# Triangular inverses by 32-row diagonal blocks: 32-column stationary operands and vector-engine block transposes in place of full 128-wide steps

## The chip, the cores and the metric

The kernel runs on one core of one Trainium2 chip. The metric is device time in microseconds, the median of three runs.

## What is computed

The reference chains three transformer-like blocks over 512 tokens of 1024 channels. The change lies in the second one, in its two recurrences: a chunked gated delta rule (`gdn` in the kernel) and an RWKV-7 scan (`rwkv`), each with 8 heads and chunks of 128 tokens. Cut to what matters:

```python
# chunk_gated_delta_rule, per head and chunk of C = 128 tokens
lower = jnp.where(strict, jnp.einsum('bhncd,bhnsd->bhncs', k_beta, k) * decay, 0.0)
t_mat = lax.linalg.triangular_solve(lower + eye, jnp.broadcast_to(eye, lower.shape),
                                    left_side=True, lower=True, unit_diagonal=True)
u = jnp.matmul(t_mat, v_beta)
w = jnp.matmul(t_mat, k_beta * jnp.exp(g_cum)[..., None])
# rwkv7_scan, per head
S = S * w_t[:, :, None, :] + sa[..., None] * b_t[:, :, None, :] + v_t[..., None] * k_t[:, :, None, :]
y_t = jnp.einsum('bhvk,bhk->bhv', S, r_t)        # sa = S a_t
```

The kernel brings the RWKV scan into the same chunked form, so both need, for each head, the inverses of four unit lower triangular 128x128 matrices I + L, one per chunk.

## The kernel before

Most of the program is linear layers. `lin` (L358) makes one 128-row output tile over 512 tokens: for each of its 128x128 weight blocks three matmuls (L368 to L370), since weights and activations are split into a high and a low part; the weight pieces come by DMA on SP and are split on ACT (L324) and DVE (L325). All work is written as calls of engines, and the framework's scheduler turns it at build time into one fixed order per engine; a section under `first()` goes ahead of other work, and two generators given to `run` are advanced in turn.

`second` (L1145) loops over j = 0 to 3, two heads each. For each j, `z.run(rwkv(...), gdn(...))` (L1231) advances the two chains in turn. Beside them the scheduler puts matmuls of `lin`: the layers of the next j (`lins`, called L1246) and gates whose results `aside` stores (L1248; 2, 1, 1 and 12 of them in j = 0 to 3). The RWKV chain has tiles `ra`, small tiles `mra` and three PSUM banks `r`; the GDN chain has `ga`, `mga` and two banks `g`.

Each chain calls `Chain.invert` (L680) once per head (L1379, L1489), so a j has four inversions and the program 16. One inversion takes `Lt`, a 128x512 tile of four transposed strictly lower matrices side by side, and leaves the four transposed inverses in `Tt`. It doubles the size b of the inverted diagonal blocks, over b = 2, 4, 8, 16, 32: a copy of the odd columns of `Lt` on ACT (L703), two matmuls with it as stationary operand (L707), a mask on DVE (L711), two matmuls with the transposed inverse as stationary operand (L714), a subtraction on DVE (L716), and then `turned`: a copy of the odd columns on ACT (L695), two transposes on TensorE (L655) and a copy out of PSUM on ACT (L659). The last step, from 64 to 128, is two groups of four 64x64 matmuls (L727, L734) with a DVE operation behind each (L730, L736).

## Time and profile before

| | |
|---|---|
| runs | 3328.02, 3328.61, 3330.11 us |
| profiled execution | 3330.9 us, of which span 3329.1 us |
| mean granted TensorE clock | 0.992 |
| busy: PE, PE weight loads, DVE, ACT, POOL | 97%, 81%, 67%, 45%, 3% |
| instructions in the span | 48326 |

The profile shows one execution. PE is TensorE's matmul stream, PEld its weight loads, which overlap with matmuls; DVE, ACT and POOL are the vector, scalar and GpSimd engines. The end of a matmul is modelled, with a tail that overlaps the next, so the time a matmul costs is read from one start to the next. One fp32 matmul leaves two records (two passes), a transpose one.

### The profile page before, as it was taken

How to read it: one execution, taken by the hardware profiler on the slowest of the kernel's cores; microseconds unless marked ns; L12 is line 12 of the kernel's file. 1: busy time of each engine (PE TensorE's matmuls, PEld its weight loads, DVE VectorE, ACT ScalarE, POOL GpSimd, SP SyncE). 2: the span in 40 equal slices, each digit the busy share in tenths (PEclk: the TensorE clock that was granted, in tenths of full speed). 3: DMA queues.
4: the chain of work that ended last, by engine and by line, in shares of the span. 5: the costliest groups of instructions: out<-in, count | busy, mean ns of one | idle time of the engine just before them, and what ended most of it. 6: DMA issues, size and time to landing. Idle time of an engine off the chain costs nothing.

```text
span 3329.1 us, 48326 instructions
## 1 busy us (share of the span) xinstructions
PE 3242.3 (97%) x19041; PEld 2700.3 (81%) x19041; DVE 2234.4 (67%) x3675; ACT 1497.2 (45%) x2491; POOL 101.0 (3%) x186
## 2 busy tenths in 40 slices
PE   7999999999999999999999999999999999999998
PEld 6778888888887887887888887888877778888887
DVE  5696645986578577566887567777687996363344
ACT  6443433432346656654332334645546665232222
POOL 0000000000000000000000000000000001000000
PEclk9999999999999999999999999999999999999999
DMA  4223333665332112125367324222227567423332
GB/s 134 64 70 98 95 117 102 215 202 161 107 103 76 46 50 73 58 64 171 122 203 242 95 81 133 69 78 92 81 80 239 171 208 239 131 88 101 95 95 76
DMA packets 128324, 393.33 MB, mean 118 GB/s; under 512 B 16056, under 2 KB 23480, under 8 KB 128096
## 3 DMA queue, kind: packets, MB, share of 16 engines
q1 hardware_dynamic: 113776, 346.82, 33.6%
q0 software_dynamic: 13168, 42.36, 3.7%
q8 instruction: 150, 2.46, 0.3%
q10 hardware_dynamic: 1152, 1.05, 0.1%
q14 instruction: 78, 0.64, 0.1%
HBM read 358.44 MB, written 31.74 MB: 117 GB/s over the span
## 4 chain that ended last, share of the span: by engine, by line
PE 88%; DVE 6%; ACT 4%; issue 2%; DMA 1%; SPq 0%; POOL 0%; DVEq 0%; ACTq 0%; POOLq 0%
PE mm L368 20%; PE mm L369 20%; PE mm L370 20%; PE mm L354 3%; PE mm L355 3%; PE mm L356 3%; PE s L2082 1%; DVE wl L325 1%; PE s L2068 1%; ACT wh L324 1%; PE r L1370 1%; PE g L655 1%; PE mm L405 1%; PE r L655 1%; PE mm L406 1%
## 5 line engine op out<-in xcount | busy, mean ns | idle before, releaser
L368 PE MATMUL mm<-h,wh 128*128 128x512 f32 x2400 | 947.6, 395 | 1.8 <-ACT t L948 1.5
L369 PE MATMUL mm<-h,wh 128*128 128x512 f32 x2400 | 948.5, 395 | 0.0
L370 PE MATMUL mm<-h,wl 128*128 128x512 f32 x2400 | 947.3, 395 | 0.0
L324 ACT ACTIVATE wh<-wr 128x1024 fp32r<-128x1024 f32 x464 | 491.4, 1061 | 949.8 <-PE mm L369 663.5
L325 DVE TENSOR_TENSOR wl<-wr,wh 128x1024 fp32r<-128x1024 f32 x464 | 567.2, 1224 | 467.6 <-ACT wh L324 462.2
L368 PEld LDWEIGHTS mm<-h,wh 128*128 128x128 f32 x2400 | 452.7, 189 | 98.4 <-issue 5.5
L370 PEld LDWEIGHTS mm<-h,wl 128*128 128x128 f32 x2400 | 452.7, 189 | 96.9 <-issue 6.0
L369 PEld LDWEIGHTS mm<-h,wh 128*128 128x128 f32 x2400 | 452.8, 189 | 96.2 <-issue 5.4
L368 PE MATMUL mm<-p,wh 128*128 128x512 f32 x599 | 233.6, 390 | 0.0
L369 PE MATMUL mm<-p,wh 128*128 128x512 f32 x599 | 233.4, 390 | 0.1
L370 PE MATMUL mm<-p,wl 128*128 128x512 f32 x599 | 233.1, 389 | 0.0
L354 PE MATMUL mm<-h,wh 128*128 128x256 f32 (+1 forms) x480 | 159.5, 344 | 14.4 <-DVE t L1930 5.3
L355 PE MATMUL mm<-h,wh 128*128 128x256 f32 (+1 forms) x480 | 160.1, 339 | 1.1 <-DVE h L569 1.0
L356 PE MATMUL mm<-h,wl 128*128 128x256 f32 (+1 forms) x480 | 158.6, 335 | 0.0
L301 DVE SCALAR_TENSOR_TENSOR ac<-wa,adas,ac 128x1024 f32<-128x1024 f32 x98 | 125.5, 1282 | 23.9 <-DMA wa<-wa 23.5
L369 PEld LDWEIGHTS mm<-p,wh 128*128 128x128 f32 x599 | 112.4, 188 | 23.9 <-DVE p L430 0.8
L368 PEld LDWEIGHTS mm<-p,wh 128*128 128x128 f32 x599 | 112.4, 188 | 23.5
L370 PEld LDWEIGHTS mm<-p,wl 128*128 128x128 f32 x599 | 112.4, 188 | 23.4
L354 PEld LDWEIGHTS mm<-h,wh 128*128 128x128 f32 x480 | 92.4, 198 | 25.8 <-ACT h L568 4.6
L355 PEld LDWEIGHTS mm<-h,wh 128*128 128x128 f32 x480 | 94.3, 198 | 10.0 <-DVE h L569 2.0
L356 PEld LDWEIGHTS mm<-h,wl 128*128 128x128 f32 x480 | 94.6, 198 | 8.5
L750 DVE SCALAR_TENSOR_TENSOR f<-mm,par,f 128x511 f32<-128x511 f32 (+1 forms) x128 | 95.5, 746 | 1.1
(661 smaller groups left out, 5244.6 us busy)
## 6 DMA issues: line engine op xcount, KB each, us to landing
wr<-w SPq DMA_DIRECT2D x464, 512.0 KB, 3.7
wa<-wa SPq DMA_DIRECT2D x96, 512.0 KB, 4.3
e<-cum SPq DMA_DIRECT2D x64, 256.0 KB, 5.1
x<-x POOLq DMA_DIRECT2D x40, 256.0 KB, 4.5
s<-ecum SPq DMA_DIRECT2D x64, 128.0 KB, 4.8
cd<-t POOLq DMA_DIRECT2D x24, 256.0 KB, 2.3
gt<-t POOLq DMA_DIRECT2D x16, 256.0 KB, 2.5
fr<-gt SPq DMA_DIRECT2D x16, 256.0 KB, 3.0
```

The source lines that it names most:

```text
L301: self.V.scalar_tensor_tensor(a, raw, s[:, k, m:m + 1], a, op0=ALU.mult, op1=ALU.add)
L324: self.A.activation(hi, raw, AF.Copy)
L325: self.V.tensor_tensor(lo, raw, hi.bitcast(F32), op=ALU.subtract)
L354: self.T.matmul(ps[:, n], lhsT=wh, rhs=x[0][k][:, n], start=k == 0, stop=False)
L355: self.T.matmul(ps[:, n], lhsT=wh, rhs=x[1][k][:, n], start=False, stop=False)
L356: self.T.matmul(ps[:, n], lhsT=wl, rhs=x[0][k][:, n], start=False, stop=k == last)
L368: self.T.matmul(out, lhsT=wh, rhs=x[0][k], start=k == 0, stop=False)
L369: self.T.matmul(out, lhsT=wh, rhs=x[1][k], start=False, stop=False)
L370: self.T.matmul(out, lhsT=wl, rhs=x[0][k], start=False, stop=k == last)
L405: self.T.matmul(ps, lhsT=a, rhs=wl, start=False, stop=False)
L655: self.z.T.transpose(ps[:, c * P:(c + 1) * P], src[:, c * P:(c + 1) * P], self.z.ident)
L750: z.V.scalar_tensor_tensor(out[:, d:], src[:, :S - d], w[:, n - 1 - d:n - d], out[:, d:], op0=ALU.mult, op1=ALU.add)
```

## The change

`invert` is written anew up to the last step. Only the four 32x32 diagonal blocks of each matrix are worked on while b goes through 2, 4, 8, 16. The blocks of all four matrices together are one 128x128 tile `Tc`, one matrix per 32 columns; `Tb` holds the same blocks, turned, as block diagonals in a 128x512 tile whose other elements were set to zero on POOL (L716). In a level `right` does four matmuls with 32 columns of `Tc` as stationary operand and 128 columns of `Lb` moving (L704), each to its own 32 partitions of PSUM; DVE turns the 32x32 blocks of the result with its own transpose (L706); `left` does four matmuls with 32 columns of that as stationary operand and `Tb` moving (L713); DVE masks (L733), turns (L734) and subtracts (L735); `turned` transposes `Tc` once on TensorE (L697) and copies it in four pieces of 32 rows into `Tb` on ACT (L699). For the step from 32 to 64 `right` is done once more, four POOL multiplies (L744) spread the blocks into the result `Tt`, which lies in the place of `Lb`, `left` is done for blocks 1 and 3 alone, two ACT copies (L749) put them into `Tt`, and a small tile `first`, made by DVE and three ACT copies (L751 to L755), is the moving operand of the first 64x64 group (L761). The two 64x64 groups stay (L761, L768). The chains get two more small tiles each (`ira`, `iga`). Line numbers of this section are those of the changed kernel, where `invert` begins 2 lines lower than before and ends 34 lines lower.

```diff
@@ -145,10 +145,12 @@
     c.add("eps_x", np.full((P, 1), 64e-5, f))
     c.add("incl", (r[None] >= r[:, None]).astype(f))
     c.add("strict", (r[None] > r[:, None]).astype(f))
-    c.add("m1", ((r[None] % 2 == 1) & (r[:, None] == r[None] - 1)).astype(f))
-    g = np.arange(64)
-    for b in (2, 4, 8, 16, 32):
-        c.add(f"lev{b}", (r[:, None] // b == r[None] // b).astype(f))
+    l, g = r[:, None] % 32, np.arange(32)[None]
+    c.add("id32", (l == g).astype(f))
+    for b in (1, 2, 4, 8, 16):
+        c.add(f"lev{b}", ((l // b % 2 == 0) & (l // b == g // b - 1)).astype(f))
+    c.add("lev32", (r[:, None] // 32 == r[None] // 32).astype(f))
+    c.add("off32", ((r[:, None] // 32 % 2 == 0) & (r[:, None] // 32 == r[None] // 32 - 1)).astype(f))
     c.add("rs128", np.broadcast_to((np.arange(S) % 128 != 0).astype(f), (P, S)))
     rs16 = np.broadcast_to((np.arange(S) % 16 != 0).astype(f), (P, S))
     c.add("inclT", (r[None] <= r[:, None]).astype(f))
@@ -679,54 +681,86 @@
 
     def invert(self, Lt, out):
 
         z, V, A, T = self.z, self.z.V, self.z.A, self.z.T
         quad = lambda x: x.rearrange("p (u n) -> p u n", u=4)
-        Tt, Ti = self.t(), self.t()
+        cut = lambda x: x.rearrange("p (u i n) -> p u i n", u=4, i=4)
+        bc = lambda x: x.unsqueeze(1).to_broadcast([P, 4, x.shape[1]])
+        rows = [slice(32 * i, 32 * i + 32) for i in range(4)]
+        small = lambda n=P: z.tile("m" + self.sb, n)
+        Lb, Tb, Tc = self.t(), self.t(), z.tile("i" + self.sb, P)
+        Tt = Lb
         out.append(Tt)
-        bc = lambda x, n: x.unsqueeze(1).to_broadcast([P, 4, n])
-        V.tensor_tensor(quad(Tt), quad(Lt), bc(z.k("m1"), P), op=ALU.mult)
-        V.tensor_tensor(quad(Tt), bc(z.ident, P), quad(Tt), op=ALU.subtract)
-        self.transposes(Tt, Ti)
+        def turned(ps):
+            T.transpose(ps, Tc, z.ident)
+            for u in range(4):
+                A.activation(cut(Tb)[rows[u], :, u], quad(ps)[rows[u]], AF.Copy)
+        def right(ps):
+            for u in range(4):
+                T.matmul(ps[rows[u], :P], lhsT=Tc[:, rows[u]], rhs=quad(Lb)[:, u], start=True, stop=True)
+            x = small()
+            V.transpose(x, ps[:, :P])
+            return x
+        def left(ps, x, blocks=range(4)):
+            ps = ps[:, P:2 * P]
+            for i in blocks:
+                T.matmul(ps[rows[i]], lhsT=x[:, rows[i]], rhs=quad(Tb)[:, i], start=True, stop=True)
+            return ps
+        z.G.memset(Tb, 0.0)
+        V.tensor_tensor(quad(Lb), quad(Lt), bc(z.k("lev32")), op=ALU.mult)
+        y = small(256)
+        for i in range(4):
+            A.activation(quad(y[:, :P])[rows[i]], cut(Lt)[rows[i], :, i], AF.Copy)
+        V.tensor_tensor(quad(y[:, :P]), quad(y[:, :P]), bc(z.k("lev1")), op=ALU.mult)
+        V.transpose(y[:, P:], y[:, :P])
+        V.tensor_tensor(quad(Tc), bc(z.k("id32")), quad(y[:, P:]), op=ALU.subtract)
         yield
-        odd = lambda x, b: x.rearrange("p (g two b) -> p g two b", two=2, b=b)[:, :, 1, :]
-        def turned(b):
-            some = z.tile("m" + self.sb, 256)
-            A.activation(some.rearrange("p (g b) -> p g b", b=b), odd(Ti, b), AF.Copy)
-            self.transposes(some, Tt[:, :256], 2)
-        for b in (2, 4, 8, 16, 32):
-            half = Ti.rearrange("p (g two b) -> p g two b", two=2, b=b)[:, :, 0, :]
+        turned(self.bank(P))
+        for b in (2, 4, 8, 16):
             ps = self.bank()
-            low = z.tile("m" + self.sb, 256)
-            A.activation(low.rearrange("p (g b) -> p g b", b=b), odd(Lt, b), AF.Copy)
-            if b == 2:
-                turned(b)
-            for u in range(2):
-                T.matmul(ps[:, u * P:u * P + P].rearrange("p (g b) -> p g b", b=b), lhsT=low[:, u * P:u * P + P],
-                         rhs=half[:, u * P // b:(u + 1) * P // b], start=True, stop=True)
-            m = z.tile("m" + self.sb, 256)
-            two = lambda x: x.rearrange("p (u n) -> p u n", u=2)
-            V.tensor_tensor(two(m), two(ps[:, :256]), z.k(f"lev{b}").unsqueeze(1).to_broadcast([P, 2, P]), op=ALU.mult)
+            x = right(ps)
+            if b == 16:
+                V.tensor_tensor(quad(Lb), quad(Lt), bc(z.k("off32")), op=ALU.mult)
             yield
-            for u in range(2):
-                T.matmul(ps[:, 256 + u * P:384 + u * P], lhsT=Tt[:, u * P:u * P + P], rhs=m[:, u * P:u * P + P],
-                         start=True, stop=True)
-            V.tensor_tensor(half, half, ps[:, 256:].rearrange("p (g b) -> p g b", b=b), op=ALU.subtract)
+            y = small(256)
+            V.tensor_tensor(quad(y[:, :P]), quad(left(ps, x)), bc(z.k(f"lev{b}")), op=ALU.mult)
+            V.transpose(y[:, P:], y[:, :P])
+            V.tensor_tensor(Tc, Tc, y[:, P:], op=ALU.subtract)
             yield
-            if b == 32:
-                self.transposes(Ti, Tt)
-            else:
-                turned(2 * b)
-            yield
+            turned(ps[:, 256:384])
+        ps = self.bank()
+        x = right(ps)
+        y = small()
+        V.transpose(y, Tc)
+        for u in range(4):
+            z.G.tensor_tensor(cut(Tt)[:, u], z.k("lev32").rearrange("p (i n) -> p i n", i=4),
+                              quad(y)[:, u].unsqueeze(1).to_broadcast([P, 4, 32]), op=ALU.mult)
+        yield
+        ps = left(ps, x, (1, 3))
+        for i in (1, 3):
+            A.activation(cut(Tt)[rows[i - 1], :, i], quad(ps)[rows[i]], AF.Copy, scale=-1.0)
+        first, y = small(256), small()
+        V.transpose(y[rows[1]], ps[rows[1]])
+        V.memset(quad(first)[rows[0], :, 32:], 0.0)
+        A.activation(quad(first)[rows[0], :, :32], quad(Tc)[rows[0]], AF.Copy)
+        A.activation(quad(first)[rows[1], :, 32:], quad(Tc)[rows[1]], AF.Copy)
+        A.activation(quad(first)[rows[1], :, :32], quad(y)[rows[1]], AF.Copy, scale=-1.0)
+        yield
 
         e, o = slice(0, 64), slice(64, P)
         ps = self.bank(256)
         for u in range(4):
-            T.matmul(ps[o, 64 * u:64 * u + 64], lhsT=Lt[e, u * P + 64:u * P + P], rhs=Ti[e, u * P:u * P + 64],
+            T.matmul(ps[o, 64 * u:64 * u + 64], lhsT=Lt[e, u * P + 64:u * P + P], rhs=first[e, 64 * u:64 * u + 64],
                      start=True, stop=True)
-        m = z.tile("m" + self.sb, 256)
+        m = small(256)
         V.tensor_scalar(m[o], ps[o], -1.0, None, op0=ALU.mult)
         yield
         ps = self.bank(256)
@@ -1148,7 +1182,7 @@
     ch = lambda x: x.rearrange("p (c n) -> p c n", c=4)
     gt = z.new([P, 16 * S], tag="gt", pool=z.dr)
     yo = z.new([P, 6 * S], tag="yo", pool=z.dr)
-    with z.phase({"r": 3, "g": 2}, fr=6, fg=8, q=6, ra=12, ga=10, vz=(1, 1024), cra=(2, 1024), cga=(2, 1024), lw=(1, 384), lx=(1, 768), mra=(4, 256), mga=(4, 256), t=2):
+    with z.phase({"r": 3, "g": 2}, fr=6, fg=8, q=6, ra=12, ga=10, vz=(1, 1024), cra=(2, 1024), cga=(2, 1024), lw=(1, 384), lx=(1, 768), mra=(4, 256), mga=(4, 256), ira=(2, 128), iga=(2, 128), t=2):
         omu = z.new([P, 15], tag="omu")
         V.tensor_scalar(omu, z.q("mu_2"), -1.0, 1.0, op0=mult, op1=add)
 
```

On PE, in the middle of the inversions of j = 0 (tiles `g_` and `r_` are PSUM banks of the GDN and the RWKV chain, `mm_` those of `lin`), stood before:

```order
L707 MATMUL r_8637<-ra_8459,mra_8638 128x128 x2
L369 MATMUL mm_9329<-h_4691,wh_9259 128x512
L655 MATMUL g_8653<-con_64,mga_8651 128x128 x2
L370 MATMUL mm_9329<-h_4690,wl_9260 128x512
L707 MATMUL r_8644<-ra_8469,mra_8645 128x128 x2
L655 MATMUL g_8659<-con_64,mga_8657 128x128 x2
L714 MATMUL r_8637<-mra_8642,ra_8458 128x128 x2
L714 MATMUL r_8644<-mra_8649,ra_8468 128x128 x2
L707 MATMUL g_8669<-ga_8317,mga_8670 128x128 x2
```

And now, with four chains' levels beside each other:

```order
L704 MATMUL g_8677<-ga_8315,iga_8317 32x128 x4
L697 MATMUL g_8587<-con_64,iga_8381 128x128
L372 MATMUL mm_9440<-h_4697,wl_9371 128x512
L697 MATMUL r_8620<-con_64,ira_8475 128x128
L704 MATMUL r_8703<-ra_8473,ira_8475 32x128 x4
L713 MATMUL g_8677<-ga_8316,mga_8682 32x128
L704 MATMUL g_8690<-ga_8379,iga_8381 32x128 x4
L713 MATMUL g_8677<-ga_8316,mga_8682 32x128 x3
L370 MATMUL mm_9440<-h_4699,wh_9370 128x512
L371 MATMUL mm_9440<-h_4700,wh_9370 128x512
```

The pairs of 128x128 matmuls became groups of four with a 32-column stationary operand, with single 128x128 transposes (L697) and `lin` (L370 to L372 now) between them; one group is cut in two by another.

Behind the last `right` of the first GDN inversion of j = 0 PE now does this up to the first 64x64 group (L761):

```order
L704 MATMUL g_8759<-ga_8315,iga_8317 32x128 x4
L372 MATMUL mm_9474<-h_4691,wl_9410 128x512
L697 MATMUL r_8703<-con_64,ira_8475 128x128
L704 MATMUL g_8777<-ga_8379,iga_8381 32x128 x4
L704 MATMUL r_8795<-ra_8473,ira_8475 32x128 x4
L697 MATMUL r_8715<-con_64,ira_8488 128x128
L713 MATMUL g_8759<-ga_8316,mga_8764 32x128 x2
L370 MATMUL mm_9474<-h_4693,wh_9409 128x512
L704 MATMUL r_8807<-ra_8486,ira_8488 32x128 x4
L713 MATMUL g_8777<-ga_8380,mga_8782 32x128 x2
L371 MATMUL mm_9474<-h_4694,wh_9409 128x512
L713 MATMUL r_8795<-ra_8474,mra_8800 32x128 x4
```
```order
L713 MATMUL r_8807<-ra_8487,mra_8812 32x128 x4
L372 MATMUL mm_9474<-h_4693,wl_9410 128x512
L370 MATMUL mm_9474<-h_4695,wh_9409 128x512
L371 MATMUL mm_9474<-h_4696,wh_9409 128x512
L761 MATMUL g_8852<-mga_8818,ga_8304 64x64 x4
```

The two pieces follow each other; L761 stands behind three `lin` matmuls, and its moving operand is `mga_8818`, the tile `first`.

On ACT, at the same place, with what each row waits for (two inversions, result tiles `ga_8315` and `ga_8379`, tiles `first` `mga_8818` and `mga_8829`), the order is now:

```order
L749 ACTIVATE ga_8315<-g_8759 32x4x32 [waits DVE_49,PE_49,Pool_49]
L749 ACTIVATE ga_8315<-g_8759 32x4x32
L749 ACTIVATE ga_8379<-g_8777 32x4x32 [waits DVE_49,PE_49,Pool_49]
L753 ACTIVATE mga_8818<-iga_8317 32x4x32
L754 ACTIVATE mga_8818<-iga_8317 32x4x32
L755 ACTIVATE mga_8818<-mga_8819 32x4x32 [waits DVE_49]
L749 ACTIVATE ga_8379<-g_8777 32x4x32
L753 ACTIVATE mga_8829<-iga_8381 32x4x32
```

These rows are new; the third, of the second inversion, waits for POOL and stands ahead of the three that make the first inversion's `first`.

## Rows read from the trace of the kernel before

**Rows 1.** The page's first part: span, then busy time, share and instructions of each engine.

```profile
span 3329.1 us, 48326 instructions
PE 3242.3 (97%) x19041; PEld 2700.3 (81%) x19041; DVE 2234.4 (67%) x3675; ACT 1497.2 (45%) x2491; POOL 101.0 (3%) x186
```

**Rows 2.** The page's chain that ended last, as shares of the span by engine and by line.

```profile
PE 88%; DVE 6%; ACT 4%; issue 2%; DMA 1%; SPq 0%; POOL 0%; DVEq 0%; ACTq 0%; POOLq 0%
PE mm L368 20%; PE mm L369 20%; PE mm L370 20%; PE mm L354 3%; PE mm L355 3%; PE mm L356 3%; PE s L2082 1%; DVE wl L325 1%; PE s L2068 1%; ACT wh L324 1%; PE r L1370 1%; PE g L655 1%; PE mm L405 1%; PE r L655 1%; PE mm L406 1%
```

**Rows 3.** Busy time of each engine in stretches: the inversions of j = 0, a stretch between those of j = 0 and j = 1, and the inversions of j = 1, 2 and 3. The columns stand in the first row.

```profile
core 0: us, PE busy (x) PEld busy (x) DVE busy (x) ACT busy (x) POOL busy (x), PEclk, DMA share, GB/s
...
1080.00:1115.00 35.00, 35.00 (x304) 32.49 (x302) 20.80 (x51) 17.19 (x45) 0.00 (x0) 1.00 0.00 1
1140.00:1180.00 40.00, 37.69 (x163) 29.83 (x162) 29.01 (x49) 24.61 (x40) 1.62 (x3) 0.91 0.26 78
1200.00:1240.00 40.00, 39.95 (x324) 36.29 (x323) 22.59 (x50) 24.06 (x63) 0.00 (x0) 1.00 0.11 34
1330.00:1375.00 45.00, 44.97 (x383) 41.22 (x380) 25.93 (x60) 24.80 (x63) 0.54 (x1) 1.00 0.10 30
1450.00:1490.00 40.00, 39.92 (x335) 36.22 (x334) 23.27 (x55) 22.38 (x59) 0.54 (x1) 1.00 0.06 21
```

**Rows 4.** PE's timeline at three places: start, duration of the whole group, engine, line, operation, tiles, shape, records in the group.

```profile
1076.83 0.43 PE L655 MATMUL r<-con,mra 128*128 128x128 f32 x2
1077.10 0.38 PE L655 MATMUL g<-con,mga 128*128 128x128 f32 x2
...
1084.92 1.24 PE L714 MATMUL r<-mra,ra 128*128 128x128 f32 x8
...
1112.39 1.05 PE L677 MATMUL r<-cra,ra 128*128 128x128 f32 x8
```

**Rows 5.** PE's timeline around a group of 32-column matmuls in the third block, the weight loads of the same group, and the line's own answer (duration min/median/max in ns, first and last start in us).

```profile
2126.30 0.28 PE L406 MATMUL mm<-wh,hc 128*128 128x256 f32 x1
2126.42 0.28 PE L404 MATMUL mm<-wh,hc 128*128 128x256 f32 x1
2126.63 0.46 PE L1799 MATMUL two<-a,a 128*32 128x32 f32 x32
2127.01 0.39 PE L405 MATMUL mm<-wl,hc 128*128 128x256 f32 x1
2127.24 0.28 PE L406 MATMUL mm<-wh,hc 128*128 128x256 f32 x1
2127.36 0.28 PE L404 MATMUL mm<-wh,hc 128*128 128x256 f32 x1
...
2126.62 0.35 PEld L1799 LDWEIGHTS two<-a,a 128*32 128x32 f32 x32
...
L1799 PEld LDWEIGHTS two<-a,a x640: 106/113/113, 2126.6 to 2470.0; 128*32 128x32 f32 x160
L1799 PE MATMUL two<-a,a x640: 196/196/217, 2126.6 to 2470.0; 128*32 128x32 f32 x160
```

**Rows 6.** PE's timeline in the third block where full 128x128 passes (L2068) and 64-column ones (L2082) alternate.

```profile
2542.17 0.71 PE L2068 MATMUL s<-c,st 128*128 128x128 f32 x4
2542.82 0.43 PE L2082 MATMUL s<-e,g 128*64 128x128 f32 x2
2543.18 1.38 PE L2068 MATMUL s<-c,st 128*128 128x128 f32 x10
...
2545.50 1.74 PE L2082 MATMUL s<-e,g 128*64 128x128 f32 x26
```

**Rows 7.** Groups of instructions between 1000 and 1500 us, shapes kept apart: line, engine, operation, tiles, shapes, count, then busy us, mean ns of one, and idle time before them with what ended it.

```profile
L714 PEld LDWEIGHTS r<-mra,ra 128*128 128x128 f32 x160 | 21.2, 191 | 2.7 <-issue 0.6 <-ACT mra L703 0.5 <-DVE mra L711 0.2
...
L711 DVE TENSOR_TENSOR mra<-r,con 128x256 f32<-128x256 f32 x40 | 17.0, 425 | 26.9 <-PE r L707 20.6 <-ACT mga L703 4.0 <-ACT ga L659 1.9
...
L716 DVE TENSOR_TENSOR ra<-ra,r 128x256 f32<-128x256 f32 x40 | 16.8, 421 | 6.7 <-PE r L714 5.6 <-ACT mra L695 0.3
...
L687 DVE TENSOR_TENSOR ra<-ra,con 128x512 f32<-128x512 f32 x8 | 5.5, 686 | 0.0
```

**Rows 8.** Answers for single lines elsewhere in the program: duration min/median/max in ns, first and last start, shapes; and one row of the groups of lines.

```profile
L542 DVE TENSOR_SCALAR f<-con,nw x32: 279/284/288, 12.6 to 3321.3; 128x128 f32<-128x128 f32 x32
...
L1482 DVE SCALAR_TENSOR_TENSOR ga<-g,q,ga x32: 341/344/352, 1031.8 to 1431.0; 128x128 f32<-128x128 f32 x32
...
L1318 ACT ACTIVATE lx<-lw x4: 310/312/313, 973.4 to 1290.8; 32x128 fp32r<-32x128 f32 x4
...
L492 POOL TENSOR_TENSOR f<-f,f x7: 724/728/1659, 13.1 to 19.0; 128x256 f32<-128x256 f32 x7
...
L2107 POOL MEMSET const-float32-0.0<- 128x1 f32 x1 | 0.1, 99 | 0.2 <-issue 0.2
```

**Rows 9.** The timeline of all engines within one level of the RWKV chain, j = 0.

```profile
1079.17 0.62 PE L707 MATMUL r<-ra,mra 128*128 128x128 f32 x4
...
1079.83 0.42 DVE L711 TENSOR_TENSOR mra<-r,con 128x256 f32<-128x256 f32 x1 [1.32 <-PE r L707]
...
1080.17 0.41 DVE L716 TENSOR_TENSOR ra<-ra,r 128x256 f32<-128x256 f32 x1
...
1080.40 0.68 PE L714 MATMUL r<-mra,ra 128*128 128x128 f32 x4
...
1080.67 0.42 ACT L695 ACTIVATE mra<-ra 128x256 f32<-128x256 f32 x1 [0.58 <-DVE ra L716]
```

**Rows 10.** PE's timeline around an idle time between two j.

```profile
1141.80 0.39 PE L370 MATMUL mm<-h,wl 128*128 128x512 f32 x1
1142.03 0.39 PE L368 MATMUL mm<-h,wh 128*128 128x512 f32 x1
1143.48 0.50 PE L616 MATMUL r<-ra,bd64r 128*128 128x512 f32 x1 [1.07 <-ACT ra L1289]
1143.82 1.69 PE L1323 MATMUL r<-q,lx 128*128 128x512 f32 x4
1145.43 0.80 PE L369 MATMUL mm<-h,wh 128*128 128x512 f32 x1
1146.03 0.63 PE L370 MATMUL mm<-h,wl 128*128 128x512 f32 x1
```

## The prediction

> **What bounds the kernel now.** I read the header of the profile first: TensorE (PE) is busy 97% of the span, the vector engine (DVE) 67%, ACT 45%, POOL 3% [rows 1]. The chain of waits says the same: 88% of what ends last is PE, three fifths of the span the three matmul lines of `lin`, only 6% DVE and 4% ACT [rows 2]. Then the stretches that hold inversions, one per j from 1080 us on: PE is busy 35.00 of 35.00, 39.95 of 40.00, 44.97 of 45.00 and 39.92 of 40.00 us, DVE and ACT 50 to 65% [rows 3]. So today an inversion costs the time that its matmuls and transposes take on PE, and its hops through DVE and ACT lie under `lin` and the other chains. Two questions decide: what PE work leaves, and whether the hops stay covered when PE has less to do.
>
> The sum is made against the profiled execution, 3330.9 us (span 3329.1); the median of the runs, 3328.61, is 2.3 lower. A measurement of this kernel tells about 0.2%, 6.7 us, from no change.
>
> **PE passes removed.** Each fp32 128x128 matmul is two passes, each transpose one; eight passes take 1.05 us, of which the last one's modelled tail is about .28, so a pass is (1.05-.275)/7 = .111 [rows 4]; two transposes, .38 to .43, fit .110. An inversion loses 20 matmuls and 18 transposes: 20x2x.111 + 18x.110 = 6.42 us. Sixteen inversions (4 j, two chains, two each): -102.7.
>
> **PE passes added.** Ten groups of 32-column matmuls (five `right`, five `left`, the last of two blocks) and five transposes. 32 matmuls with 32 columns occupy .46 us, .264 without the last one's tail of .196: .033 per round of four, less than a tenth of what 32 would take one after another; their 32 weight loads take .35 us together [rows 5]. Column groups run side by side, and so do their loads. 26 matmuls of 64 columns and N=128 take 1.74 us: 13 rounds of two passes at .109 wide [rows 6]. A group of four with N=128 is thus 2x.109. Per inversion 20x.109 + 5x.110 = 2.73; times 16, and 1.5 for a dozen groups that the order cuts in two: +45.2. The upper end, groups run one after another, is a rival below.
>
> The Trainium skill ("TensorEngine Tiling (Array Packing)", Restrictions) says that column tiling turns fast weight load off, which speaks against 32-column stationary operands. The trace agrees on the single load: the 32-column one lasts 113 ns, against 191 for four times the columns [rows 5, 7]. By that rule with the four loads in a row a group would cost about .45 instead of .22, some 37 us over the program, an estimate from these rows; the 32 loads in .35 us say that they overlap, so the sum has nothing for it.
>
> **Changes of shape.** Between 128-column and narrower matmuls PE loses time: four full passes between two narrow groups take .65 us from start to start, against 4x.111 (+.20), and the narrow pair after them .36 against .22 (+.14) [rows 6]. Around the 32-column group the last 256-column matmul ahead takes .21 to the next start where .12 is usual (+.09), the group .38 against 8x.033 (+.12), and the first matmul behind it .23 against .12 (+.11) [rows 5]. So in and out together cost .32 to .34 in both places: .16 per change. On PE's order the number of such changes rises from 383 to 616: 233 x .16 = +37.3. This takes back nearly two thirds of the saving.
>
> PE work: -102.7 + 45.2 + 37.3 = **-20.2 us**.
>
> **First instructions of groups.** Two transposes that wait for ACT take .43 where two that follow another pair take .38 [rows 4]; four 128x128 matmuls with a wait in the middle show 1.24 against 1.05 for eight passes. At .05 per group, the lower of these, before has 16 groups per inversion (three per level, one at the end), 12.8 us. After, the narrow groups have this in their change of shape; the 80 turns keep .05. **-8.8.**
>
> **Work on DVE and ACT.** Removed on DVE: two 512-wide operations (.68) and ten 256-wide (.42), 5.6 us per inversion [rows 7]. Added: again two 512-wide, and about 21 narrow ones. Stream transposes don't occur in the trace; between a 128x128 TENSOR_SCALAR (.284) and a 256-wide operation (.425) I take .345, a 128x128 operation that reads PSUM [rows 8]. That gives about 8.5 us per inversion, +2.9. DVE has 40% idle in these stretches, so it costs nothing there by itself. ACT's fifteen wide copies become 29 copies of 32 rows, .31 alone [rows 8], perhaps .19 each in a queue: also a draw, but in one chain. With PE to DVE .04, DVE to PE .15 and DVE to ACT .09 [rows 9] a level needs: right .22, transpose .345, left .22, three DVE operations .97, turn .15, four ACT copies .95, hops and changes of shape about 1.1: 3.95 us. For j=0 to 2 the order has 75 to 114 `lin` matmuls (.225 apart [rows 10]) in an inversion's stretch, PE 5 to 8 us per level: covered. In j=3 there are only 9 (29 before), and the last levels hold 3.1 us of PE work: .8 short, four times: **+3**. Other tight hops: **+2** (0 to 6).
>
> **The wait for POOL.** The new POOL multiplies write the block diagonal into the result, four per inversion, over `Lb`, so they wait for the last `right`. In ACT's order the copies of the second inversion (L749), which wait for POOL, stand ahead of L753 to L755, which build `first` for the first inversion. So the first L761 waits for eight multiplies. The nearest rows are a 128x256 multiply on POOL, .728, and a 128x1 memset, .099 [rows 8]: with a fixed part of .1 a 128x128 is .41, bounds .36 (half) and .73 (nothing saved); with the .1 that lies between POOL instructions, .5. From the end of the last `right`: DVE 1.1, POOL 8x.5 = 4.0, ACT with its hop 1.2: 6.3 us. Between that `right` and L761 PE has, in the order shown for j=0, six `lin` (1.36), seven groups (1.5), two turns (.2) and four visits to narrow shape (1.3): 4.4. Short by 1.8, in j=1 by 1.6, j=3 by 3.6, in j=2 nothing since L749 stands later there. The RWKV chains, whose eight multiplies start with less ahead of them (5.2), lack .2, .8, .8 and 1.3. **+10.1**. Behind the waiting L749 only those chains' own copies are queued; PE itself stands, since it runs its order. After idles of about a microsecond PE's granted clock falls: the matmul behind a 1.07 us idle takes .63 to .80 where .39 is usual [rows 10], and the stretch with two such idles has .91 over 40 us [rows 3], 3.6 us lost, 1.8 for each. Two long waits: **+3.6**.
>
> The Trainium skill ("GPSIMD Engine Reference", Elementwise) has 4497 ns for a 2048-element two-input operation, 2.2 ns each, so .28 for 128, an estimate. The row here is 2.8 ns each and decides. By the page's figure the waits for POOL would come to about 4 us and the whole to 3310.
>
> **Queues.** SP issues the same transfers. On POOL's queue the memsets of `Tb` stand ahead of the DMAs (L1502) that the GDN chain's second inversion is built from, and a `gt` store behind the multiplies; POOL is 3% busy [rows 1] and these DMAs are issued while PE has the first head's matmuls before it. I cost this at nothing; without that cover a 512-wide memset, between .1 and four times .73, delays a load by at most 2.9 us, once per j: upper end +12, kept for the range.
>
> **Sum:** -20.2 -8.8 +3 +2 +10.1 +3.6 = -10.3: 3320.6 in the profiled execution, **3318.3** as a median.
>
> **Rivals.** *POOL becomes the bound (slower).* If a 128x128 multiply costs what the 256-wide one does, .73, each of the seven waits grows by 8x.32 = 2.5 us, 18 in all, and three more pass a microsecond, 5 us of clock: -10.3 + 23 = +13, 3342. It decides from about .55 per multiply. For it: the first of these operations took 1.659 [rows 8], so POOL has a large variable part. Against: two points only suggest a fixed part of .1.
> *All covered.* The E1 waits fall under `lin` that comes late, and the hops too: -29, 3300. For it: DVE and ACT hardly hold PE up today [rows 2]. Against: the order is fixed at build and PE stands at L761.
> *All given back.* A multiply near .55, or 8 more hops of a microsecond: 3328.
> *Column groups one after another (slower).* 160 groups x 2 passes x 3 x .109 = +105: 3423. Against: rows 5 and 6, whose form differs only in N.
>
> **How the numbers follow.** Forecast .50 (its own range 3309 to 3327), POOL .15, covered .18, given back .14, one after another .03. Faster by over 0.2%: .38 of the forecast, all of "covered", .02: .58. Within: .11, .10, .01: .22. Slower: .01, .02, .14, .03: .20. The range 3299 to 3336 leaves out the lower half of "covered" and most of the two slower cases, .2.
>
> **What would show it.** Right: groups of L704 or L713 that follow each other about .22 us apart, DVE operations of .35 at the stream transposes, PE's idle share up by 15 to 20 us, largest before L761 and in j=3, with L744 at about .41 and L749 waiting for it. Wrong: L744 at .3 or .7; groups of four at .8; a change of shape far from .16; or waits of PE at L704, L713 and L697 in j=0 to 2, where I count none.

## The result and the profile after

The changed kernel takes 3352.05 us (median of four, 3350.78 to 3355.03) against 3329.36 for the kernel before: ratio 1.0071, interval 1.0056 to 1.0086. It is **slower by 22.7 us**; forecast was 11 us faster, and 3352 lies above the range. The profiled execution is 3355.0 us, span 3353.3.

What a single operation costs came out close. From the groups of lines between 1000 and 1540 us (count | busy us, mean ns | idle before):

```profile
L699 ACT ACTIVATE ga<-g 32x128 f32<-32x128 f32 x160 | 42.9, 268 | 25.5 <-PE g L697 22.1
L706 DVE STREAM_TRANSPOSE mga<-g 128x128 f32<-128x128 f32 x40 | 12.4, 312 | 31.2 <-PE g L704 30.9
L744 POOL TENSOR_TENSOR ga<-con,mga 128x128 f32<-128x128 f32 x32 | 12.0, 408 | 94.9 <-DVE mga L742 94.9
L733 DVE TENSOR_TENSOR mga<-g,con 128x128 f32<-128x128 f32 x32 | 8.4, 280 | 8.6 <-PE g L713 8.5
```

They answer to [rows 7, 8]: POOL's multiply .408 (I took .41), the stream transpose .312 (.345), the mask .280. The .28 that the prediction worked out, as an estimate, from the Trainium skill ("GPSIMD Engine Reference", Elementwise) is too low here: the measurement decides. The ACT copy of 32 rows takes .268, not .19.

PE's work fell as foreseen. I split the stretch from 1000 us to the start of the third block's first layer (a point both kernels pass with the same work done) into PE's idle gaps, half of its busy time at the low granted clock (0.5, which is 1.2 GHz), and the rest, which is PE's work at full clock:

| us | before | after |
|---|---|---|
| length | 586.2 | 609.2 |
| PE's work at full clock | 564.6 | 538.9 |
| idle | 13.3 | 41.2 |
| lost to the low clock | 8.3 | 29.1 |

So 25.7 us of work went and 48.7 us of waiting came. The second row also holds waits too short to show as idle: later runs with the same PE instructions (e1, e2, e6, e9, e11, e12, e13, e17) have 536 to 546 us there, so the 25.7 are good to some 8 us. Where the waiting came, the windows over the inversions of j = 0 to 3 show (first to last matmul of `invert`; columns as in rows 3); first the kernel before, then the changed one:

```profile
1056.90:1111.70 54.80, 54.80 (x432) 49.33 (x431) 35.55 (x77) 30.61 (x76) 0.00 (x0) 1.00 0.10 31
1193.90:1246.80 52.90, 52.85 (x427) 47.74 (x426) 31.50 (x69) 29.88 (x75) 0.54 (x1) 1.00 0.09 26
1321.20:1371.80 50.60, 50.57 (x413) 45.59 (x412) 30.78 (x70) 30.20 (x75) 1.08 (x2) 1.00 0.14 43
1438.50:1487.70 49.20, 49.10 (x406) 44.37 (x405) 27.83 (x64) 27.89 (x72) 0.54 (x1) 1.00 0.11 38
```
```profile
1050.10:1119.20 69.10, 66.35 (x608) 45.38 (x608) 50.58 (x143) 43.24 (x129) 7.10 (x18) 1.00 0.18 58
1196.50:1256.40 59.90, 57.53 (x569) 37.97 (x569) 40.54 (x130) 36.96 (x120) 5.98 (x16) 1.00 0.13 39
1329.60:1387.30 57.70, 54.52 (x552) 36.86 (x552) 38.85 (x126) 37.79 (x122) 8.64 (x21) 1.00 0.17 51
1452.90:1511.50 58.60, 52.07 (x495) 36.48 (x495) 33.46 (x114) 33.17 (x115) 5.97 (x16) 0.72 0.04 10
```

Before, 207.5 us with PE hardly ever idle; after, 245.3 us (242.0 if both are counted from their first product, L707 and L704): **each stretch got longer**, although less inversion work stands in it. What fills j = 0 to 2 is `lin`: 114, 75 and 70 matmuls instead of 55, 42 and 36. In j = 3 there are 9 instead of 29, and behind it 285 instead of 346. Of the 48.7 us, 8.3 stand in the stretches of j = 0 to 2, 22.1 in that of j = 3 (6.5 idle, the rest lost to the clock), 12.3 behind it. Behind the last stretch both kernels need the same time to the end of the block (98.6 and 97.7 us), so the end of j = 3's stretch, 1487.7 against 1511.5, is the whole loss.

What a level waits for is seen on ACT's timeline in j = 2 (start, duration of the group, operation, records, [idle before]):

```profile
1344.95 0.60 ACT L661 ACTIVATE cra<-r 128x512 f32<-128x512 f32 x1 [3.59 <-PE r L657]
1346.70 0.60 ACT L1427 ACTIVATE cra<-r 128x512 f32<-128x512 f32 x1 [1.15 <-PE r L1425]
1347.19 2.30 ACT L699 ACTIVATE ga<-g 32x128 f32<-32x128 f32 x8
1349.52 0.60 ACT L661 ACTIVATE ra<-r 128x512 f32<-128x512 f32 x1
1350.14 1.06 ACT L326 ACTIVATE wh<-wr 128x1024 fp32r<-128x1024 f32 x1
1351.10 0.58 ACT L661 ACTIVATE ra<-r 128x512 f32<-128x512 f32 x1
1351.58 0.59 ACT L982 ACTIVATE t<-mm 128x512 f32<-128x512 f32 x1
1352.06 2.31 ACT L699 ACTIVATE ra<-r 32x128 f32<-32x128 f32 x8
1354.39 2.32 ACT L699 ACTIVATE ga<-g 32x128 f32<-32x128 f32 x8
1356.74 2.32 ACT L699 ACTIVATE ra<-r 32x128 f32<-32x128 f32 x8
1361.93 1.15 ACT L699 ACTIVATE ga<-g 32x128 f32<-32x128 f32 x4 [2.87 <-PE g L697]
```

The two inversions of a chain go side by side: eight copies, 2.3 us, per level, and the GDN chain's next eight come 7.2 us later (1347.19, 1354.39), and again 7.5 later. Here `lin` stands between the levels, so 7.2 us is not the chain's own need. In j = 3 hardly any is left, and from 1475.3 to 1492.4 us the granted clock is 1.00:

```profile
1476.84 2.31 ACT L699 ACTIVATE ra<-r 32x128 f32<-32x128 f32 x8
1479.64 2.32 ACT L699 ACTIVATE ga<-g 32x128 f32<-32x128 f32 x8 [0.50 <-PE g L697]
1481.99 2.32 ACT L699 ACTIVATE ra<-r 32x128 f32<-32x128 f32 x8
1485.47 2.32 ACT L699 ACTIVATE ga<-g 32x128 f32<-32x128 f32 x8 [1.16 <-PE g L697]
1487.81 2.32 ACT L699 ACTIVATE ra<-r 32x128 f32<-32x128 f32 x8
```

A chain's eight copies come 5.2 to 5.8 us apart, and the copies of both chains take 4.6 us of that on ACT. I had 3.95 us for a level. PE's waits (engine, line waited for: us, times, longest) name the same place, and the tail behind j = 3:

```profile
PE g L704 <- ACT ga L699: 9.6, 29, 1.1
PE mm L370 <- ACT ra L431: 7.2, 1, 7.2
PE r L618 <- ACT ra L1323: 6.7, 5, 2.4
PE g L657 <- DVE ga L1516: 4.8, 1, 4.8
...
PE g L761 <- ACT mga L755: 1.9, 2, 1.8
...
PE r L761 <- ACT mra L755: 1.0, 3, 0.5
```

### The profile page after: what moved, and what is told of

Read it like the earlier page. It is cut to its first block, busy times and chain, and to the rows that moved or that the text cites. A ratio compares the mean times of both kernels' runs of the same rounds, so it can differ in the third digit from the quotient of the medians.

```text
span 3353.3 us, 49569 instructions
## 1 busy us (share of the span) xinstructions
PE 3237.5 (97%) x19409; PEld 2644.4 (79%) x19409; DVE 2251.9 (67%) x3883; ACT 1523.7 (45%) x2683; POOL 133.2 (4%) x266
## 5 line engine op out<-in xcount | busy, mean ns | idle before, releaser
L370 PE MATMUL mm<-h,wh 128*128 128x512 f32 x2400 | 947.5, 395 | 1.8 <-ACT t L982 1.5
L372 PE MATMUL mm<-h,wl 128*128 128x512 f32 x2400 | 948.3, 395 | 0.0
L370 PEld LDWEIGHTS mm<-h,wh 128*128 128x128 f32 x2400 | 452.6, 189 | 101.4 <-issue 8.8
L372 PEld LDWEIGHTS mm<-h,wl 128*128 128x128 f32 x2400 | 452.5, 189 | 101.0 <-issue 10.4
L370 PE MATMUL mm<-p,wh 128*128 128x512 f32 x599 | 233.6, 390 | 0.0
L372 PE MATMUL mm<-p,wl 128*128 128x512 f32 x599 | 233.0, 389 | 0.0
L372 PEld LDWEIGHTS mm<-p,wl 128*128 128x128 f32 x599 | 112.4, 188 | 23.3
L370 PEld LDWEIGHTS mm<-p,wh 128*128 128x128 f32 x599 | 112.4, 188 | 23.3
```

The lines of the kernel that those rows point to most:

```text
L370: self.T.matmul(out, lhsT=wh, rhs=x[0][k], start=k == 0, stop=False)
L372: self.T.matmul(out, lhsT=wl, rhs=x[0][k], start=False, stop=k == last)
```

## The experiments

Each was timed beside the kernel before on its chip. Times are medians; "stretches" is the sum of the four, "ahead" the `lin` matmuls that PE does between the start of j = 0's first inversion and that of j = 3. The kernel before took 3326.1 to 3329.4 us there. The runs that the argument leans on most stand in a table at the end. Every edit also changes the order that is fixed at build.

**Is it the stock of `lin` matmuls?** My first theory after the result: the stock is finite, j = 0 to 2 use it up, and j = 3 stands bare at the low clock.

```diff
-for _, o in zip(range((2, 1, 1, 12)[j]), gates):
+for _, o in zip(range((0, 0, 0, 16)[j]), gates):   # e1;  (1, 0, 0, 15): e2;  before.py with (8, 8, 0, 0): e3
```

> The changed kernel with the sixteen gate layers all behind j = 3 (0, 0, 0, 16 in place of 2, 1, 1, 12): the same work, but the order now has 73 lin matmuls beside the inversions of j = 3 where the changed kernel has 9. Stock theory (the lin matmuls beside the inversions are a fixed stock; the changed kernel spends it in j = 0 to 2 and PE stands bare, at the low clock, from 1440 us to 1551): the idle time and the low clock of j = 3 (23.7 and 22.9 us in that stretch) shrink by half or more, 3320 to 3335 us. Rival, hops (the narrow steps' own waits on ACT, DVE and POOL cost the time wherever they stand): within 6 us of the changed kernel, 3346 to 3358.

> The changed kernel with 1, 0, 0, 15 gate layers: 39 lin matmuls beside the inversions of j = 3. Stock theory: between the changed kernel and the one with 73, some 3330 to 3345 us, with the low clock in j = 3 between theirs. Rival, hops: 3346 to 3358, as before the edit.

> The kernel before, with its old inversions, and 8, 8, 0, 0 gate layers: its order has 9 lin matmuls beside the inversions of j = 3 where the kernel before has 29, and none left behind them. Stock theory: the same idle time and low clock in j = 3 as the changed kernel shows, without the 25 us that the new inversion saves on PE: 3350 to 3375 us. Rival, hops: the old inversion has few hops, so 3325 to 3338.

e1 3349.5, e2 3345.2: e1 lies in the rival's numbers, e2 just between the two. The rows of j = 3's stretch, e1 and then e2:

```profile
1448.40:1507.00 58.60, 56.34 (x552) 36.70 (x553) 38.06 (x121) 37.04 (x121) 8.61 (x21) 1.00 0.17 51
```
```profile
1445.40:1503.70 58.30, 52.10 (x525) 34.99 (x525) 36.52 (x120) 34.92 (x118) 6.50 (x17) 0.91 0.09 26
```

With 73 `lin` matmuls at the full clock, 39 at 0.91, or 9 at 0.72 in the changed kernel, the stretch takes 58.6, 58.3 and 58.6 us: **giving j = 3 its `lin` matmuls back does not shorten it**. It is not shown by this that PE and its clock do not count there. In e1 `lin` stands where the low clock stood (PE is busy 56.3 of 58.6 us), and in the changed kernel PE is busy nearly all of the time at the low clock:

```profile
1448.00:1475.30 27.30, 25.70 (x151) 18.85 (x151) 14.96 (x45) 14.04 (x43) 0.00 (x0) 0.50 0.07 20
```

e3, slower by 37 us, lies in the stock theory's numbers. Its stretches are short (212.5), but PE does 81 more matmuls ahead of j = 3 (18 us) and the gaps between the stretches grow from 223 to 257 us; in the last gap, with 26 `lin` matmuls instead of 165, PE idles 19.1 us and loses 12.6 at the low clock. So matmuls placed ahead of a chain delay it and are missing later. In the changed kernel, putting them back where they were missing brought only 3 to 7 us.

**Would more PE work help?**

```diff
+if j == 3:   # behind the gate layers
+    for n in range(3):
+        idle = z.bank("mm")
+        for k in range(24):
+            z.T.matmul(idle, lhsT=z.onesr, rhs=h[0][k % 8], start=k == 0, stop=k == 23)
```

> The changed kernel with 72 matmuls more (128x512, three PSUM tiles of 24, results not used) behind the gate layers of j = 3: 16.4 us of PE work at the full clock that nothing needs. The order puts 46 of them beside the inversions of j = 3 and 25 shortly ahead. Stock theory: they fill idle time and hold the clock up, so the kernel gets faster though it does more: 3325 to 3345 us. Rival, hops: waits stay and the matmuls come on top, 3352 to 3370.

3346.3: 16 us of work more and 5.8 us faster, just outside both theories' numbers. The time at the low clock fell from 71.7 to 30.7 us, and j = 3's stretch to 55.0, all of it at the full clock:

```profile
1450.90:1505.90 55.00, 52.12 (x542) 34.53 (x541) 34.94 (x120) 33.41 (x116) 5.96 (x16) 1.00 0.04 11
```

The gain is net of the work that was added, so it is no upper bound on what the clock costs. But 16.9 us of the loss are left with j = 3 at the full clock.

**What makes the chain long?** Operations were left out:

```diff
-for u in range(4):                      # e5, e6: in turned
+for u in range(1):
     A.activation(cut(Tb)[rows[u], :, u], quad(ps)[rows[u]], AF.Copy)
-V.tensor_tensor(quad(y[:, :P]), quad(left(ps, x)), bc(z.k(f"lev{b}")), op=ALU.mult)   # e5
-V.transpose(y[:, P:], y[:, :P])
+V.transpose(y[:, P:], left(ps, x))
-for u in range(4):                      # e8
-    z.G.tensor_tensor(cut(Tt)[:, u], ...)
```

> The changed kernel with three of the four ACT copies of each turn (L699) and the mask (L733) left out, so its inverses are not the reference's; every matmul and transpose on PE stays. Hops theory (the copies and the mask make each level's chain longer than its PE work, the order fills the stretch with lin matmuls, and these are then missing at the end): 49 lin matmuls are left beside the inversions of j = 3, the four inversion stretches shrink from 245 us to about 215, 3312 to 3332 us. Rival, narrow matmuls (their changes of shape and small waits on PE cost the time): PE's work is the same, 3345 to 3355.

> The changed kernel with three of the four ACT copies of each turn left out, the mask kept (inverses not the reference's). Hops theory: part of the way, 51 lin matmuls left for j = 3, 3325 to 3342 us. Rival, narrow matmuls: 3345 to 3355. Rival, DVE alone is what makes the chain long: within 4 us of the changed kernel.

> The changed kernel with the four POOL multiplies per inversion (L744) left out, so the result lacks its diagonal blocks. Hops theory: PE waits only 2.9 us at L761 in the changed kernel, and 9 lin matmuls are left for j = 3 as before the edit: 3346 to 3354 us. Rival POOL of the prediction (L761 waits for POOL): 3335 to 3342.

e6 3319.1, e5 3311.8 (both faster than the hops theory's numbers), e8 3349.2. With one copy instead of four the kernel is 33 us faster, faster than before (ratio .9977, .9968 to .9986), with every PE instruction in place. The mask is worth 7 more, the multiplies on POOL at most 3, which is within the spread of e8's runs. e6's stretches, rows as above:

```profile
1048.60:1111.90 63.30, 62.71 (x600) 44.28 (x600) 48.46 (x142) 25.94 (x68) 7.39 (x17) 1.00 0.17 50
1183.20:1236.90 53.70, 53.37 (x555) 37.02 (x553) 39.59 (x128) 21.06 (x61) 6.50 (x17) 1.00 0.12 40
1308.90:1360.30 51.40, 49.93 (x544) 34.61 (x544) 37.62 (x127) 20.14 (x61) 8.00 (x18) 1.00 0.14 45
1426.40:1478.40 52.00, 49.70 (x529) 34.90 (x529) 36.22 (x122) 18.99 (x59) 6.88 (x18) 0.95 0.13 42
```

220 us instead of 245, ACT 86 us busy instead of 151, DVE as before the edit. The stretches hold more `lin` matmuls than the changed kernel's (286, not 268), but PE idles or loses to the low clock 7 us in them instead of 31. The narrow matmuls and their changes of shape, rival in e5 and e6, are out as the cause of the loss.

**Latency or load?** Do the copies count because a level waits for four in a row, or because ACT is shared?

```diff
+# e9: the other three from z.ident, e13: from Tc (96 columns), into a scratch tile
+for u in range(1, 4):
+    A.activation(z.tile("kk", 96)[rows[u]], Tc[rows[u], :96], AF.Copy)
 # e12: one copy by ACT, four by POOL
+A.activation(c[:128], ps[:128], AF.Copy)
+for u in range(4):
+    z.G.tensor_copy(cut(Tb)[rows[u], :, u], quad(c)[rows[u]])
```

> As e6_one_copy (one of the four ACT copies of a turn is made, inverses not the reference's), but the three others are made too, of the same shape, from a constant into a scratch tile that nothing reads: ACT does as much as in the changed kernel, and no level waits for it. fg has one tile less for room. Latency theory (the four copies count because each level's next product waits for them): within 6 us of e6_one_copy, 3315 to 3327 us. Load theory (ACT, 60% busy and shared by four inversions, has no time for 29 more instructions each): within 6 us of the changed kernel, 3345 to 3357.

> As e6_one_copy, with three more ACT copies per turn of 32 rows and 96 columns from Tc itself into a scratch tile nothing reads, so they come at the time of the turn and can't be done ahead (inverses not the reference's). ACT then does nearly what it does in the changed kernel in the same stretches, and no product waits for it. Latency theory (a level waits for the four copies in a row): as e6_one_copy, 3315 to 3327 us. Load theory (the copies of four inversions are in each other's way on ACT): 3340 to 3357.

> The changed kernel with one 128x128 ACT copy out of PSUM per turn, and the four 32-row copies into Tb made by POOL from that. The result is the same; the chain of a level gets longer (a hop and four POOL copies, some 1.2 us or more), ACT's load goes back to a quarter. Load theory: 3318 to 3335 us. Latency theory: 3352 to 3375.

e9 (3337.3) did not tell them apart: the order put the copies ahead of j = 0's inversions, which start 17 us later than e6's; from there to the end of the block it takes 528.7 us, e6 528.4. e13 kept them in the stretches: 3328.8, between e6 and the changed kernel and within neither theory's numbers.

```profile
1049.70:1116.70 67.00, 65.82 (x612) 46.27 (x611) 49.83 (x143) 43.40 (x126) 7.13 (x18) 1.00 0.19 59
1184.60:1242.00 57.40, 56.07 (x568) 37.66 (x568) 40.46 (x128) 37.84 (x118) 6.52 (x17) 1.00 0.14 44
1313.70:1367.10 53.40, 52.25 (x546) 34.68 (x546) 38.37 (x126) 38.54 (x120) 8.75 (x19) 1.00 0.15 49
1432.60:1486.90 54.30, 51.02 (x531) 33.55 (x532) 37.20 (x121) 35.72 (x116) 8.06 (x20) 0.98 0.13 41
```

Its stretches sum to 232.1 us with ACT busy 156, no less than in the changed kernel (151). With ACT loaded but nobody waiting, 23 of the 33 us come back: some two thirds latency, one third load, if the two add. e12 has one ACT copy in a turn, as e6, and a longer turn: 3385.6, above both theories' numbers, with

```profile
PE r L715 <- POOL ra L701: 22.8, 29, 1.7
PE g L715 <- POOL ga L701: 9.8, 11, 1.5
```

where L715 is `left` and L701 POOL's copies (.32 to .34 each). POOL is busy 138 us in these stretches instead of 28, so its load grew with the turn. By e13 above all, latency weighs more.

**Ways out that keep the result.**

```diff
 # e10: right of the next level ahead of turned, both in the new bank
+ps = self.bank(); x = right(ps); turned(ps[:, 256:384])
 # e11: copies 2 and 3 of a turn
+V.tensor_copy(cut(Tb)[rows[u], :, u], quad(ps)[rows[u]])
 # e7: mask ahead, on POOL
+z.G.tensor_tensor(cut(Lm), cut(Lb), <lev b, broadcast>, op=ALU.mult); x = right(ps, Lm)
 # e17, e18: weight parts while j = 0 to 3 are built
+self.G.tensor_copy(hi, raw)        # e17
+self.G.tensor_tensor(lo, raw, hi.bitcast(F32), op=ALU.subtract)   # e18
```

> The changed kernel with the mask taken out of the chain: POOL masks Lb for each level (128x512 into a tile of its own, which a product can do ahead of time), so that behind `left` only the transpose and the subtraction follow; fg and ra have one tile less each to make room. The result is the same matrix. 45 lin matmuls are left for j = 3. Hops theory: 3330 to 3344 us. Rival, narrow matmuls: 3345 to 3355. Rival, POOL: its 512-wide multiplies (about 1.6 us each, four per inversion) become the longest wait of a level: over 3355.

> The changed kernel with `right` of the next level ahead of `turned`, both in the new level's PSUM bank: the bank of a level is then not held by the four ACT copies, and L704 needs only Tc, so it need not wait for L699 (9.6 us of PE's waits in the changed kernel). The result is the same. Latency theory, with the PSUM bank as what makes `right` wait for the copies: each level loses up to 1.1 us of chain, 3325 to 3342 us. Load theory: 3345 to 3357; its order has 9 lin matmuls for j = 3, as the changed kernel's, which speaks for this.

> The changed kernel with two of the four copies of each turn on DVE, beside the two on ACT. The result is the same. Latency theory: the turn is half as long, 3330 to 3345 us. Load theory: DVE, 67% busy in the stretches, is no better off than ACT, and the order has 171 lin matmuls beside j = 0's inversions, so 3350 to 3375.

> The changed kernel, complete, with the high parts of the weights (L324 before, 1.06 us of ACT for each 24 lin matmuls) copied by POOL instead of ACT while j = 0 to 3 are built; POOL is 4% busy. ACT's load in the stretches falls by about a fifth, the four copies in a row stay. By e13 about half of the longer stretch is load and half latency: 3330 to 3344 us, 70 lin matmuls left beside the inversions of j = 3. Rival, latency alone: 3346 to 3357. Rival, POOL's copy (over 2 us each) holds up the weights: over 3360.

> The changed kernel, complete, with the low parts of the weights (L325 before, 1.22 us of DVE for each 24 lin matmuls) made by POOL instead of DVE while j = 0 to 3 are built. DVE, 67% busy in the stretches and with five operations in each level's chain, gets a fifth of its load off: 3320 to 3340 us, 60 lin matmuls left for j = 3. Rival, ACT alone is what is short: 3346 to 3357. Rival, POOL's subtraction (about 3 us each) holds up the weights: over 3360.

None won. e10, 3367.0, outside both theories' numbers: the wait for L699 moved from L704 to `left` (L713, 27 times, 11.4 us), which needs the copies in any case, so a level gets no shorter. e11, 3379.5, above both: stretches 292, with DVE busy 223 us in them instead of 163. e7, 3354.8, in the numbers of the narrow matmuls, which e6 rules out: POOL's masks take 1.12 to 1.15 us and PE waits 7.0 us for them, which may eat what the shorter chain gives. e17 and e18, 3346.6 and 3347.4, miss the numbers expected and lie in those of their first rivals. Against the kernel before on the same chip they stand at 1.0055 (1.0035 to 1.0076) and 1.0064 (1.0048 to 1.0081), the changed kernel at 1.0071: no gain clear of noise. They took little load away: the weight pieces are 10.6 of ACT's 151 us and 13.9 of DVE's 163 in the changed kernel's stretches, not a fifth, and ACT is still busy 142 us in e17's, DVE 169 in e18's.

**Fewer new inversions.** Old and new were put into one kernel; there the old one's first mask is that of 2x2 blocks, so its result differs.

```diff
+(c.invert if True else c.invert_old)(x, Tt)     # RWKV: e14;  "if j == 3" in both chains: e15;  all old: e16
```

> The new inversion in the RWKV chain alone, the old one in the GDN chain (both sets of masks; fg has one tile less for room). PE saves half of 25 us; ACT's copies of the new kind are half. Theory now held (stretches grow where four new inversions run beside each other; 58, 51, 46 and 14 lin matmuls in its order, near the kernel before): 3312 to 3326 us. Rival, each new inversion costs its share alone: half of the changed kernel's loss, 3337 to 3343.

> The new inversion in j = 3 alone, the old one in j = 0 to 2 (both sets of masks; fg has one tile less). The order has 72 lin matmuls beside the inversions of j = 3. Stock theory: the longer stretch of j = 3 is filled and its 6 us of PE work saved, but less is left for the tail behind it: 3322 to 3336 us. Rival, the new inversion is slower wherever it stands: 3337 to 3345.

> The old inversion everywhere, with the second set of masks and fg one tile less, as the ground that e14 and e15 stand on. All theories: within 5 us of the kernel before, 3323 to 3334 us.

e16 3328.7, e15 3329.5, e14 3339.7 (the rival's numbers). With new inversions in one chain alone the stretches are the shortest of all, 182 us, 26 less than e16's. The theory held was wrong on e14 all the same, and not by the rival's mechanism: the order put 81 more `lin` matmuls ahead of j = 3 (18 us), the gaps between the stretches grew from 218 to 257, and j = 3 ended 11 us later. It is e3's loss again. e15 is as fast as e16, in the stock theory's numbers. Its stretch of j = 3 is 59.6 us instead of 49.1, with 72 `lin` matmuls in it instead of 30, the others are unchanged, and its gaps are 3 us shorter: a longer stretch cost nothing measurable where work that had to be done anyway filled it.

| | median | stretches | between them | ahead | end of j = 3 | to the block's end |
|---|---|---|---|---|---|---|
| before | 3329 | 207.5 | 223.3 | 695 | 1487.7 | 98.6 |
| after | 3352 | 245.3 | 216.1 | 797 | 1511.5 | 97.7 |
| e1 | 3350 | 252.4 | 205.1 | 730 | 1507.0 | 97.5 |
| e3 | 3367 | 212.5 | 257.1 | 776 | 1524.0 | 97.2 |
| e5 | 3312 | 212.3 | 209.2 | 724 | 1470.9 | 97.5 |
| e6 | 3319 | 220.3 | 209.4 | 755 | 1478.4 | 98.6 |
| e11 | 3380 | 292.1 | 194.9 | 797 | 1537.0 | 96.5 |
| e12 | 3386 | 289.1 | 202.7 | 754 | 1540.7 | 98.3 |
| e13 | 3329 | 232.1 | 205.1 | 754 | 1486.9 | 98.6 |
| e14 | 3340 | 182.2 | 256.7 | 774 | 1495.4 | 100.8 |
| e16 | 3329 | 208.6 | 218.4 | 693 | 1484.1 | 99.8 |

## Why the prediction was wrong

- **PE's work**, -20.2 and -8.8: right, 25.7 us measured, within some 8. Groups of four follow each other .24 apart (.22), and the change of shape is there: a `lin` matmul ahead of a narrow group takes .32 to the next start instead of .23, the first one behind it .34, the last narrow one .20 instead of .11, together some .3 more for in and out (the sum had .32). The reading of the weight loads does not hold: 32, 64 and 128 columns take 113, 136 and 191 ns in the kernel before (L1799, L2082, L714), which lie on one line, so they show no faster path that narrow loads would miss. The sum had nothing for it.
- **The wait for POOL**, +10.1: too large. PE waits 2.9 us at L761, e8 gives 3. The path was right and the single multiply was priced right, but eight in a row were not. In j = 0:

```profile
1095.42 0.43 PE L704 MATMUL g<-ga,iga 128*32 128x128 f32 x8 [0.49 <-ACT ga L699]
1096.85 2.98 POOL L744 TENSOR_TENSOR ga<-con,mga 128x128 f32<-128x128 f32 x8 [1.66 <-DVE mga L742]
1100.90 0.68 PE L761 MATMUL g<-mga,ga 64*64 64x64 f32 x8 [0.16 <-ACT mga L755]
```

  They take 2.98 us, .37 apart, and not 4.0; from the end of `right` to L761 5.05 us pass, not 6.3, and PE waits .16. The rival in which POOL becomes the bound is out: the kernel is slower, but not by it.
- **The step that failed** is the sentence that for j = 0 to 2 the hops are "covered", with "3.95 us" for a level and "+3" for j = 3. That sum let each inversion have ACT and DVE for itself. Four run beside each other: a chain's copies come eight in a row, 2.3 us, where the sum had .95 for four, the two chains' in turn, on an ACT that also makes weights and evacuates PSUM, and where hardly any `lin` stands between, a level takes 5.2 to 5.8 us. And a covered hop was counted as free: the `lin` matmuls that cover j = 0 to 2, 259 instead of 133, are for the most part taken from j = 3 and from behind it. The sum had 18.7 us of idle time and low clock (3, 2, 10.1 and 3.6); there are 48.7, of which 22.1 in j = 3's stretch alone. The sign that the prediction named for this is there: PE waits 7.3 us at L704 for L699 in j = 0 to 2, where it counted none. That the copies are what costs, e6 shows: one instead of four, every PE instruction in place, and 33 us come back.
- **The clock**, +3.6: 20.8 us more are lost at the low level. The longest low stretch, 1448.0 to 1475.3 us, follows an idle of 4.8 us, in which PE waits for the GDN chain (L657, above). An idle of about a microsecond is not always followed by one: behind the 1.26 us at 1284.9 in the kernel before the granted clock stays at 1.00. So the low clock comes behind waits, but once there it costs time of its own; how much is open, since e4's 5.8 us are net of the added work.
- **The single copy** on ACT was mis-sized, .27 to .29 in a queue instead of .19 (four take 1.15, not .95), which alone, by the prediction's own sum, would not have changed the sign. The old inversion has seventeen wide copies, not fifteen; nothing in the sum hangs on it.

What stays open: how the third that e13 leaves to load divides between the engines; what the low clock costs by itself; and how much of each difference is the chain and how much the order that the scheduler makes for it (the stretches of the new inversion hold 240 to 393 `lin` matmuls), since no run changed the chain under a held order. Whether another order would let e14's short stretches count was not tried. A complete kernel that beats both was not found.

## What to carry to other kernels

A PE that is 97% busy may hide a serial chain that is just as long; before PE work is taken out, add up the chain with every user of each engine that runs beside it, since what PE saves beyond the chain's slack comes back as idle time. Work that covers a wait is not free when the stretch gets longer: it is drawn from later, and put ahead of a chain it delays it. One wide copy that becomes four narrow ones counts four times in a level's latency; and a low clock that follows idle time points first at the wait ahead of it.

## What the runs showed of the hardware

Four 32-column fp32 matmuls with N = 128 take .24 us together, their starts 7 ns apart. A stream transpose of 128x128 fp32 takes .31 us on DVE out of PSUM and .28 out of SBUF, a POOL multiply of 128x128 .41 (eight in a row .37 apart) and of 128x512 1.12 to 1.15, so its cost is not in proportion to the width, and a POOL copy of 32x128 .32 to .34, more than ACT's .27. An ACT copy out of PSUM takes .27 for 32x128 and .28 for 128x128 (e12): four copies of 32 rows cost four times one of 128. 16 us of matmuls that nothing needs made a kernel 6 us faster (e4).
